# Softmax weights scaled in place and turned by TensorE's transpose mode, in place of products with diagonal matrices

## The chip, the cores and the metric

The kernel runs on one core of a Trainium2 chip. The metric is the device time of one execution, in microseconds (us), as the median over runs. The engines are named as the profile names them: PE is TensorE (PEld its weight loads), DVE is VectorE, ACT is ScalarE, POOL is GpSimd, SP is SyncE, which issues the DMAs.

## What is computed

The reference is one decoder layer on 512 tokens of width 1024, all in float32: a recurrent branch and a sparse-attention branch are merged by gates, and a convolutional feed-forward part and a gated embedding follow. The change touches the attention alone, whose core, cut, is

```python
logits = jnp.einsum('btngd,btknd->btngk', qg, k_sel).astype(jnp.float32) * (HEAD_DIM ** -0.5)
logits = logits + bias.astype(jnp.float32)
logits = jnp.where((dist >= 0)[:, :, None, None, :], logits, -jnp.inf)
probs = jax.nn.softmax(logits, axis=-1).astype(v.dtype)
o = jnp.einsum('btngk,btknd->btngd', probs, v_sel)
```

There are eight heads of 128 channels; four heads share one head of keys and values. Of the keys that are not later than a query only the 128 with the best index scores take part; the kernel keeps all 512 keys and adds a large negative mask to the others.

## The kernel before

Activations lie with channels on the 128 partitions and the 512 tokens along the free dimension. A weight matrix is streamed as tiles of 128x1024 (`load`, line 85) and split into a rounded part and a remainder (`split`, line 90: ACT casts `raw` to `whi`, DVE subtracts to `wlo`). Each product of two float32 matrices is then three passes in the reduced type float32r (`three`, line 97). A weight tile makes one output tile `acc` of 128x512 by 8 x 3 = 24 such products (`mm`, line 102); they are called wide products below. `pair` (line 112) splits an activation in the same way: ACT casts, DVE subtracts.

The attention is interleaved with these weight products. `attn(s)` hands to step s, ahead of its weight products, the turn of head s - 1 and the scores of head s, and in their midst the value product of head s - 1. The steps are the last three of the query projection and then those of the second gate (`b_step`, line 404, whose results `gb` get a sigmoid on ACT).

Per head there are these parts:

- `qk` (line 359). For each block b of 128 queries the scores against the 128(b + 1) keys up to it go to a PSUM tile `aux` (three products). DVE multiplies by the query's scale and adds the bias (line 369), then adds the mask and takes the row maximum (line 371), all into the tile `E`, in which the four blocks lie side by side with 128, 256, 384 and 512 columns. ACT takes the exponential with the negated maximum and sums the row (line 376); DVE takes the reciprocal of the sums (line 377). Line 380 then makes four diagonal matrices `dg`: the identity scaled, row by row, by these reciprocals.
- `turn` (line 382). The value product needs the weights with keys on the partitions. Each of the ten 128x128 blocks of `E` is loaded as the stationary operand and multiplied in float32 by the diagonal matrix of its query block, which turns it and normalises it at once. The results fill three PSUM tiles; `pair` splits them into `PT` (lines 115 and 116).
- `pv` (line 394). Twelve products of values and `PT`; `pair` writes the head's output into `QO`.

A scheduler sets the order of the instructions on each engine: it takes the program's order as priority and places an instruction where it takes its inputs to be ready. Every engine then works through its queue in that order. ACT loads a function table where the next function (exponential or sigmoid) is not in the loaded one. The tile `E` has two buffers, `dg` and `PT` have one, and PSUM has five tiles for `aux`.

The lines with two products per block are these:

```python
nc.tensor.matmul(a[:, c:c + 128], E[h][:, SEG[b] + 128 * j:SEG[b] + 128 * j + 128], dg[:, b],
                 start=True, stop=True)
```

Of the kernel before, what the change touches and what calls it, by code (L numbers as in the profile page):

```python
# [10 lines left out]
F32 = mybir.dt.float32  # L11
# [8 lines left out]
NB = 4  # L20
# [22 lines left out]
SEG = [0, 128, 384, 768]  # L43
# [4 lines left out]
def layer(ctx: ExitStack, tc: tile.TileContext, xT, pT, wall, vwi, vec, relb, onehot, out):  # L48
    nc = tc.nc
# [13 lines left out]
    ident = base.tile([128, 128], F32, name="ident")  # L63
# [10 lines left out]
    def aux_tile():  # L74
        return psum.tile([128, T], F32, name="aux", bufs=5)
# [21 lines left out]
    def three(o, lh, ll, rh, rl, start, stop):  # L97
        nc.tensor.matmul(o, lh, rh, start=start, stop=False)  # L98
        nc.tensor.matmul(o, lh, rl, start=False, stop=False)  # L99
        nc.tensor.matmul(o, ll, rh, start=False, stop=stop)  # L100
# [11 lines left out]
    def pair(dst, src, g=None, lo=None):  # L112

        if g is None:
            nc.scalar.copy(dst[:, 0], src)
            nc.vector.tensor_sub(dst[:, 1], src, dst[:, 0].bitcast(F32))
        else:
            nc.scalar.activation(dst[:, 0], src, AF.Copy, scale=g)
            nc.vector.scalar_tensor_tensor(dst[:, 1], src, g, dst[:, 0].bitcast(F32),
                                           op0=OP.mult, op1=OP.subtract)  # L120
# [42 lines left out]
    P = {}  # L163
# [180 lines left out]
        nc.scalar.activation(s, s, AF.Sqrt, bias=epsc[:, 1:2])  # L344
        nc.vector.reciprocal(s, s)

    G, E, DG, PT = {}, {}, {}, {}

    def spread_bias(h):
        nc.sync.dma_start(bias_d[h], bv_d[h:h + 1].to_broadcast([128, 640]))  # L350
# [8 lines left out]
    def qk(h):  # L359
        n = h // 4  # L360
        E[h] = P["pool"].tile([128, 1280], F32, name="E", bufs=2)
        sm = pm.tile([128, 4, 4], F32, name="sm", bufs=2)
        for b in range(NB):
            w = 128 * (b + 1)
            s = slice(b * 128, b * 128 + 128)
            a = aux_tile()[:, :w]
            three(a, QO[:, h, 0, s], QO[:, h, 1, s], KK[:, n, 0, :w], KK[:, n, 1, :w], True, True)
            e = E[h][:, SEG[b]:SEG[b] + w]
            nc.vector.scalar_tensor_tensor(e, a, qs[:, h, b:b + 1], G[h][:, 128 * (3 - b):128 * (3 - b) + w],
                                           op0=OP.mult, op1=OP.add)  # L370
            nc.vector.tensor_tensor_reduce(e, e, mask[:, SEG[b]:SEG[b] + w], 1.0, SENT, OP.add, OP.max,
                                           sm[:, 0, b:b + 1])
        nc.vector.tensor_scalar_mul(sm[:, 1], sm[:, 0], -1.0)
        for b in range(NB):
            e = E[h][:, SEG[b]:SEG[b] + 128 * (b + 1)]
            nc.scalar.activation(e, e, AF.Exp, bias=sm[:, 1, b:b + 1], accum_out=sm[:, 2, b:b + 1])
        nc.vector.reciprocal(sm[:, 3], sm[:, 2])
        DG[h] = P["pool"].tile([128, NB, 128], F32, name="dg", bufs=1)
        for b in range(NB):
            nc.vector.tensor_scalar_mul(DG[h][:, b], ident, sm[:, 3, b:b + 1])  # L380

    def turn(h):
        dg = DG[h]
        PT[h] = P["pool"].tile([128, 2, 1280], F32R, name="PT", bufs=1)
        for js, o, n in (((0,), 0, 512), ((1, 3), 512, 512), ((2,), 1024, 256)):
            a = aux_tile()
            for j in js:
                for b in range(j, NB):
                    c = PTO[j] - o + 128 * (b - j)
                    nc.tensor.matmul(a[:, c:c + 128], E[h][:, SEG[b] + 128 * j:SEG[b] + 128 * j + 128], dg[:, b],  # L390
                                     start=True, stop=True)
            pair(PT[h][:, :, o:o + n], a[:, :n])

    def pv(h):
# [232 lines left out]
    def attn(s):  # L627
        pre, ex = [], []
        if 0 <= s - 1 < HEADS:
            if s == 1:  # L630
                ex.append((4, lambda: turn(0)))
            else:
                pre.append(lambda: turn(s - 1))
            ex.append((6, lambda: pv(s - 1)))
        if 0 <= s < HEADS:
            pre.append(lambda: qk(s))
            ex.append((7, lambda: load_bias(s + 2)))
        return pre, ex
# [232 lines left out]
```

## Time and profile before

| | us |
|---|---|
| median of 3 runs | 949.13 |
| lowest and highest | 948.16, 949.47 |
| the profiled execution | 947.85 |
| its span, first to last instruction | 946.1 |
| PE busy | 931.9 |
| DVE busy | 575.1 |
| ACT busy | 435.4 |

A busy share is an average over the whole kernel. The place of the change is a stretch of some 90 us, from about 313 to 403 us. In a timeline each row has its start, its duration, engine, line, operation, tiles, shape and count; an "x20" merges 20 instructions that follow one another. A duration on PE reaches from the start of a product to its modelled end, which overlaps the next; the pace is read from the starts. A float32 product leaves two records, and a float32r product one.

### The profile page before, as it was taken

The page shows a single profiled execution, that of the slowest core. Times are in us where ns is not written, and L with a number is a line of the kernel's source. Part 1 is how long each engine was busy: PE and PEld are TensorE (multiplying, and loading weights), DVE is VectorE, ACT ScalarE, POOL GpSimd, SP SyncE. Part 2 cuts the span into 40 slices and gives each one's busy share as a digit, 9 for nine tenths or more (in the row PEclk, how much of TensorE's full clock was granted, in tenths as well). Part 3 has the DMA queues.
Part 4 walks back from the last instruction along what each step waited for, and adds up shares of the span by engine and source line. Part 5 has one row for each costly group of instructions (what it writes and reads, how often), then busy time and mean ns, then how long its engine had stood idle before and what let it go on. Part 6 is the DMA issues. An engine that isn't in the chain of part 4 may idle for free.

```text
span 946.1 us, 11256 instructions
## 1 busy us (share of the span) xinstructions
PE 931.9 (99%) x4332; PEld 776.9 (82%) x4332; DVE 575.1 (61%) x916; ACT 435.4 (46%) x624; POOL 40.5 (4%) x44
## 2 busy tenths in 40 slices
PE   7899999999999999999999999999999999999998
PEld 5788878888888888888888888888888888888886
DVE  6769699689983857735566555555555543332373
ACT  6557876995222557742344433333333322222341
POOL 2000000000000000000000111111111100000000
PEclk9999999999999999999999999999999999999999
DMA  7561123114333311123442323223223223223242
GB/s 266 175 223 52 65 89 116 63 68 134 112 112 94 118 45 56 46 89 95 150 133 97 104 90 102 99 89 105 96 89 109 92 89 111 90 90 111 100 144 89
DMA packets 31317, 99.31 MB, mean 105 GB/s; under 512 B 3480, under 2 KB 3992, under 8 KB 31264
## 3 DMA queue, kind: packets, MB, share of 16 engines
q1 hardware_dynamic: 31248, 98.58, 31.5%
q8 instruction: 34, 0.56, 0.3%
q14 instruction: 19, 0.16, 0.1%
q10 hardware_dynamic: 16, 0.02, 0.0%
HBM read 94.37 MB, written 6.84 MB: 107 GB/s over the span
## 4 chain that ended last, share of the span: by engine, by line
PE 93%; DVE 3%; ACT 3%; DMA 1%; issue 0%; SPq 0%; DVEq 0%
PE acc L98 28%; PE acc L100 28%; PE acc L99 28%; PE aux L390 2%; PE aux L98 1%; PE aux L100 1%; PE aux L99 1%; PE aux L337 1%; DMA F<-in_xT 1%; DVE rstd L426 1%; ACT ri L269 1%; DVE tmp L548 1%; DVE XN L554 0%; PE aux L214 0%; PE aux L213 0%
## 5 line engine op out<-in xcount | busy, mean ns | idle before, releaser
L94 ACT CAST whi<-raw 128x1024 fp32r<-128x1024 f32 (+1 forms) x157 | 164.2, 1046 | 360.0 <-PE acc L99 281.6
L95 DVE TENSOR_TENSOR wlo<-raw,whi 128x1024 fp32r<-128x1024 f32 (+1 forms) x157 | 191.0, 1217 | 96.3 <-ACT whi L94 95.1
L98 PE MATMUL acc<-XN,whi 128*128 128x512 f32 x504 | 197.4, 392 | 0.0
L100 PE MATMUL acc<-XN,wlo 128*128 128x512 f32 x504 | 196.9, 391 | 0.0
L99 PE MATMUL acc<-XN,whi 128*128 128x512 f32 x504 | 196.9, 391 | 0.0
L100 PE MATMUL acc<-XG,wlo 128*128 128x512 f32 (+1 forms) x456 | 175.8, 386 | 0.0
L98 PE MATMUL acc<-XG,whi 128*128 128x512 f32 (+1 forms) x456 | 175.8, 386 | 0.0
L99 PE MATMUL acc<-XG,whi 128*128 128x512 f32 (+1 forms) x456 | 175.8, 386 | 0.0
L100 PEld LDWEIGHTS acc<-XN,wlo 128*128 128x128 f32 x504 | 94.7, 188 | 20.7 <-DVE wlo L95 1.0
L98 PEld LDWEIGHTS acc<-XN,whi 128*128 128x128 f32 x504 | 94.7, 188 | 18.7
L99 PEld LDWEIGHTS acc<-XN,whi 128*128 128x128 f32 x504 | 94.7, 188 | 18.6
L99 PEld LDWEIGHTS acc<-XG,whi 128*128 128x128 f32 x456 | 85.7, 188 | 17.3
L98 PEld LDWEIGHTS acc<-XG,whi 128*128 128x128 f32 x456 | 85.7, 188 | 17.1
L100 PEld LDWEIGHTS acc<-XG,wlo 128*128 128x128 f32 x456 | 85.7, 188 | 17.0
L464 DVE TENSOR_TENSOR gp<-acc,rstd 128x512 f32<-128x512 f32 x24 | 16.6, 693 | 60.2 <-PE acc L100 60.1
L100 PE MATMUL acc<-H,wlo 128*128 128x512 f32 x128 | 49.8, 389 | 0.0
L98 PE MATMUL acc<-H,whi 128*128 128x512 f32 x128 | 49.8, 389 | 0.0
L99 PE MATMUL acc<-H,whi 128*128 128x512 f32 x128 | 49.8, 389 | 0.0
L477 DVE TENSOR_TENSOR tmp<-tmp,acc 128x512 f32<-128x512 f32 x24 | 16.5, 688 | 47.3 <-POOL tmp L470 47.3
L470 POOL TENSOR_TENSOR tmp<-tmp,rstd 128x512 f32<-128x512 f32 x24 | 30.8, 1282 | 273.5 <-ACT tmp L469 273.5
L469 ACT ACTIVATE tmp<-tmp 128x512 f32<-128x512 f32 x24 | 15.2, 632 | 47.1 <-DVE tmp L468 47.1
L468 DVE SCALAR_TENSOR_TENSOR tmp<-gp,vc,tmp 128x512 f32<-128x512 f32 x48 | 36.0, 749 | 0.8
(218 smaller groups left out, 1223.2 us busy)
## 6 DMA issues: line engine op xcount, KB each, us to landing
raw<-in_wall SPq DMA_DIRECT2D x154, 512.0 KB, 3.3
bias_d<-bv_d SPq DMA_DIRECT2D x8, 320.0 KB, 5.9
F<-in_xT SPq DMA_DIRECT2D x8, 256.0 KB, 5.4
proj_d<-pst SPq DMA_DIRECT2D x4, 512.0 KB, 3.7
bias<-bias_d SPq DMA_DIRECT2D x8, 256.0 KB, 2.7
tmp<-in_xT SPq DMA_DIRECT2D x8, 256.0 KB, 3.7
tmp<-proj_d SPq DMA_DIRECT2D x8, 256.0 KB, 3.4
out_dram<-tmp SPq DMA_DIRECT2D x7, 256.0 KB, 2.5
```

The source lines that it names most:

```text
L94: nc.scalar.copy(HI[i][:, :n], RAW[i][:, :n])
L95: LAST[0] = nc.vector.tensor_sub(LO[i][:, :n], RAW[i][:, :n], HI[i][:, :n].bitcast(F32))
L98: nc.tensor.matmul(o, lh, rh, start=start, stop=False)
L99: nc.tensor.matmul(o, lh, rl, start=False, stop=False)
L100: nc.tensor.matmul(o, ll, rh, start=False, stop=stop)
L269: nc.scalar.activation(dst[m], a, AF.Sigmoid, bias=col(b0 + m))
L390: nc.tensor.matmul(a[:, c:c + 128], E[h][:, SEG[b] + 128 * j:SEG[b] + 128 * j + 128], dg[:, b], start=True, stop=True)
L464: nc.vector.tensor_mul(gp[:, 2:], a, rstd)
L468: nc.vector.scalar_tensor_tensor(t, gp[:, j:j + T], col(V_FW + 24 * j + f), t, op0=OP.mult, op1=OP.add)
L469: nc.scalar.activation(t, t, AF.Gelu_apprx_tanh)
L470: nc.gpsimd.tensor_mul(t, t, rstd)
L477: nc.vector.tensor_mul(t, GL[f], a)
```

## The change

`qk` no longer makes diagonal matrices. It multiplies each block of `E` by the reciprocals in place. `turn` then uses TensorE's transpose mode with the constant identity.

```diff
         nc.vector.reciprocal(sm[:, 3], sm[:, 2])
-        DG[h] = P["pool"].tile([128, NB, 128], F32, name="dg", bufs=1)
         for b in range(NB):
-            nc.vector.tensor_scalar_mul(DG[h][:, b], ident, sm[:, 3, b:b + 1])
+            e = E[h][:, SEG[b]:SEG[b] + 128 * (b + 1)]
+            nc.vector.tensor_scalar_mul(e, e, sm[:, 3, b:b + 1])
 
     def turn(h):
-        dg = DG[h]
...
-                    nc.tensor.matmul(a[:, c:c + 128], E[h][:, SEG[b] + 128 * j:SEG[b] + 128 * j + 128], dg[:, b],
-                                     start=True, stop=True)
+                    nc.tensor.transpose(a[:, c:c + 128], E[h][:, SEG[b] + 128 * j:SEG[b] + 128 * j + 128], ident)
```

Since the scheduler places instructions anew, the order changes in the attention stretch on PE, DVE and ACT, and nowhere else but for tile numbers. Three places follow. In each fence a row is line, operation, output <- inputs, shape of the output and, after an x, how often it stands there in a row.

DVE, from the end of the scores of head 6 on; `sm` holds maxima, sums and reciprocals. Before:

```order
L373 TENSOR_SCALAR sm<-sm 128x4
L377 RECIPROCAL sm<-sm 128x4
L380 TENSOR_SCALAR dg<-ident,sm 128x128 x4
L116 TENSOR_TENSOR QO<-aux,QO 128x512
L95 TENSOR_TENSOR wlo<-raw,whi 128x1024
L116 TENSOR_TENSOR PT<-aux,PT 128x512
```

And with the change:

```order
L116 TENSOR_TENSOR QO<-aux,QO 128x512
L373 TENSOR_SCALAR sm<-sm 128x4
L377 RECIPROCAL sm<-sm 128x4
L380 TENSOR_SCALAR E<-E,sm 128x128
L380 TENSOR_SCALAR E<-E,sm 128x256
L380 TENSOR_SCALAR E<-E,sm 128x384
L380 TENSOR_SCALAR E<-E,sm 128x512
L95 TENSOR_TENSOR wlo<-raw,whi 128x1024
```

The four equal scalings have become four of growing width, and the remainder of the output of head 5 (`QO`) has moved from behind them to ahead of the negated maximum.

ACT, the exponentials of head 6. Before:

```order
L115 CAST PT<-aux 128x512
L115 CAST PT<-aux 128x256
L376 ACT_TABLE_LOAD
L376 ACTIVATE E,sm<-E,sm 128x128
L376 ACTIVATE E,sm<-E,sm 128x256
L376 ACTIVATE E,sm<-E,sm 128x384
L376 ACTIVATE E,sm<-E,sm 128x512
L115 CAST QO<-aux 128x512
```

And with the change:

```order
L115 CAST PT<-aux 128x512 x2
L115 CAST PT<-aux 128x256
L115 CAST QO<-aux 128x512
L376 ACT_TABLE_LOAD
L376 ACTIVATE E,sm<-E,sm 128x128
L376 ACTIVATE E,sm<-E,sm 128x256
```

The cast of the output of head 5 stands ahead of the table load, which it followed before.

PE, the turn of head 5. Before:

```order
L98 MATMUL acc<-XN,whi 128x512
L99 MATMUL acc<-XN,whi 128x512
L390 MATMUL aux<-dg,E 128x128 x10
L98 MATMUL aux<-KK,QO 128x128
L99 MATMUL aux<-KK,QO 128x128
```

And with the change:

```order
L100 MATMUL acc<-XN,wlo 128x512
L389 MATMUL aux<-ident,E 128x128 x3
L98 MATMUL acc<-XN,whi 128x512
L389 MATMUL aux<-ident,E 128x128 x7
L98 MATMUL aux<-KK,QO 128x128
```

One wide product has come in between the turned blocks. From here to the turn of head 6 there were 25 wide products and are now 31: one within the turn, two around the scores, and 28 behind the value product, where 14 stood.

## Rows read from the trace of the kernel before

**Rows 1.** The page, busy time of each engine.

```profile
PE 931.9 (99%) x4332; PEld 776.9 (82%) x4332; DVE 575.1 (61%) x916; ACT 435.4 (46%) x624; POOL 40.5 (4%) x44
```

**Rows 2.** Windows, one head: length, busy us (instructions) PE, PEld, DVE, ACT, POOL, clock, DMA.

```profile
366.60:378.35 11.75, 11.75 (x71) 10.49 (x71) 8.39 (x23) 8.71 (x18) 0.00 (x0) 1.00 0.13 46
```

**Rows 3.** Timeline of PE, from the turn of head 4 to that of head 5.

```profile
364.97 2.39 PE L390 MATMUL aux<-dg,E 128*128 128x128 f32 x20
367.12 0.30 PE L98 MATMUL aux<-KK,QO 128*128 128x128 f32 x1
...
371.63 0.39 PE L98 MATMUL aux<-PT,V 128*128 128x512 f32 x1
...
373.21 0.22 PE L98 MATMUL aux<-PT,V 128*128 128x128 f32 x1
373.26 0.28 PE L99 MATMUL aux<-PT,V 128*128 128x128 f32 x1
...
373.49 0.44 PE L98 MATMUL acc<-XN,whi 128*128 128x512 f32 x1
...
376.73 2.39 PE L390 MATMUL aux<-dg,E 128*128 128x128 f32 x20
```

**Rows 4.** Timeline of DVE in the same stretch; in brackets idle time and what ended it.

```profile
367.69 0.89 DVE L369 SCALAR_TENSOR_TENSOR E<-aux,qs,bias 128x128 f32<-128x128 f32 x2 [0.32 <-PE aux L100]
...
369.10 1.02 DVE L116 TENSOR_TENSOR PT<-aux,PT 128x512 fp32r<-128x512 f32 x2
370.04 1.27 DVE L369 SCALAR_TENSOR_TENSOR E<-aux,qs,bias 128x384 f32<-128x384 f32 x2
...
372.43 0.17 DVE L373 TENSOR_SCALAR sm<-sm 128x4 f32<-128x4 f32 x1
374.96 0.18 DVE L377 RECIPROCAL sm<-sm 128x4 f32<-128x4 f32 x1 [2.36 <-ACT E L376]
375.17 0.87 DVE L380 TENSOR_SCALAR dg<-ident,sm 128x128 f32<-128x128 f32 x4
```

**Rows 5.** Timeline of ACT in the same stretch.

```profile
369.35 1.28 ACT L376 ACT_TABLE_LOAD   x1
...
374.83 0.56 ACT L115 CAST QO<-aux 128x512 fp32r<-128x512 f32 x1
375.30 0.57 ACT L409 COPY gb<-acc 128x512 f32<-128x512 f32 x1
375.78 1.04 ACT L94 CAST whi<-raw 128x1024 fp32r<-128x1024 f32 x1
```

**Rows 6.** Timeline of PE, turn of head 0 and the statistics products behind it.

```profile
318.25 2.39 PE L390 MATMUL aux<-dg,E 128*128 128x128 f32 x20
320.48 0.95 PE L337 MATMUL aux<-ones,tmp 128*128 128x2 f32 x8
```

**Rows 7.** Groups by form, DVE, scalings by a column: busy us, mean ns of one.

```profile
L380 DVE TENSOR_SCALAR dg<-ident,sm 128x128 f32<-128x128 f32 x32 | 7.0, 282 | 0.2
...
L218 DVE TENSOR_SCALAR mask<-tmp,wi 128x512 f32<-128x512 f32 x1 | 0.5, 486 | 0.0
L218 DVE TENSOR_SCALAR mask<-tmp,wi 128x384 f32<-128x384 f32 x1 | 0.5, 451 | 0.0
...
L218 DVE TENSOR_SCALAR mask<-tmp,wi 128x256 f32<-128x256 f32 x1 | 0.4, 384 | 0.0
```

**Rows 8.** Timeline of PE at the start of the kernel.

```profile
9.01 0.63 PE L99 MATMUL acc<-QO,whi 128*128 128x512 f32 x1
9.44 0.63 PE L100 MATMUL acc<-QO,wlo 128*128 128x512 f32 x1
...
10.74 0.39 PE L98 MATMUL acc<-QO,whi 128*128 128x512 f32 x1
10.97 0.39 PE L99 MATMUL acc<-QO,whi 128*128 128x512 f32 x1
```

**Rows 9.** Timeline of DVE, the diagonal matrices of head 1.

```profile
323.26 0.87 DVE L380 TENSOR_SCALAR dg<-ident,sm 128x128 f32<-128x128 f32 x4
```

More of the change, by code (lines that the diff above doesn't have):

```diff
@@ L345, in q_scale @@
         nc.vector.reciprocal(s, s)
-    G, E, DG, PT = {}, {}, {}, {}
+    G, E, PT = {}, {}, {}
     def spread_bias(h):
```

## The prediction

> **What bounds the kernel now.** I read the page first: TensorE is busy 931.9 of 946.1 us [rows 1]. A change can therefore pay only by shortening TensorE's queue, and whatever it lays on another engine costs only where TensorE comes to wait for it. Next the stretch of the edited lines, the attention heads, which run from about 318 to 403 us between the ordinary weight products. The window view of one whole head [rows 2] shows TensorE busy 11.75 of 11.75 us at granted clock 1.00 (the 2.4 GHz level), VectorE 8.39, ScalarE 8.71. So a head lasts as long as its TensorE work. The timeline [rows 3] confirms it: the block turns of heads 4 and 5 start at 364.97 and 376.73, 11.76 apart, with nothing idle between them.
>
> What hides behind that is a chain which the reader should follow in [rows 4] and [rows 5]. A score product enters VectorE (367.69); the sums and maxima end with the negated maximum (372.43); ScalarE's exponentials take until the reciprocal (374.96, 2.53 later); the four diagonal tiles run from 375.17 to 376.04; the turn that needs them starts at 376.73. The spare time is 0.69 us, the number this change plays with.
>
> **The change, part by part.**
>
> *Products removed.* Ten 128x128 blocks a head are turned, and each costs two records today: 20 records from 376.73, and 2.15 us for the same 20 between 364.97 and 367.12 [rows 3], so 0.1075 us a record and 0.215 a block. The changed program, built, holds 4252 matmuls and as many weight loads, 80 of each fewer than the 4332 of [rows 1]: one pass for each of the 80 blocks instead of two. What such a pass costs no row shows. From above: 0.215, if one pass is as long as the two. From below: 0.055, the distance at which one 128-column product follows another (373.21 and 373.26, [rows 3]). In between lies the row that is most alike, today's own record: a new 128-column load for each product, 0.1075. That loads and not columns set that pace is seen in the statistics products, which stream two columns and still need 0.95 us for eight [rows 6]. I take 0.1075: 80 x (0.215 - 0.1075) = **8.6 us** off TensorE's queue, 1.08 a head.
>
> The Trainium skill, "TensorE: Matmul & The Clock Gate", section Terms, says that the transpose mode makes float32 four times faster. By it a block would cost an estimated 0.054 us and the term would be 12.9 us; the trace of before has no transpose that could confirm it.
>
> *Scaling moved.* The four diagonal tiles, 0.87 us a head [rows 4], go; four in-place scalings of 128, 256, 384 and 512 columns come. Their nearest rows are the scalings by a column of weights: 384, 451 and 486 ns at 256, 384 and 512 columns [rows 7]. With 0.28 for the narrow one that makes 1.60. Today's four of 0.282 end within 0.87, so they overlap by about 0.085 at each of three joints; less that, 1.35 us, 0.48 more than before. Lower bound: no growth. Upper bound: the pace of the two-input sums of the same widths, 0.89 + 1.27 [rows 4], 2.16 less overlap, about 1.93. VectorE has 3.4 us a head free [rows 2], so its load costs nothing; the 0.48 lies on the chain.
>
> *Order moved.* The scheduler puts the heads further apart: between the turns of heads 5 and 6 stand 31 wide products instead of 25, so a head's TensorE time becomes 11.76 - 1.08 + 6 x 0.23 = 12.06 us (0.23: 10.74 to 10.97, [rows 8]). Those products are only moved, not added. ScalarE now casts the attention output ahead of the exponentials and loads their table between the two. In before that load (369.35, 1.28 us [rows 5]) sat in idle time; now it is on the chain.
>
> *Where a wait could come.* I walk head 6 from the first turned block of head 5 (t = 0). The ten blocks and one wide product end at 1.31. VectorE takes the first score 0.57 after that product's start (367.12 to 367.69), at 1.88. Then come 1.41 for the narrow sums and maxima, 0.6 and 0.94 for the three PT remainders, 2.39 for the wide sums and maxima, 0.6 for the output's remainder [rows 4] (0.6 is my share for a 512-wide one of the two that take 1.02): 7.8. ScalarE: the value product ends 28 wide products before the next turn, 12.06 - 6.4 = 5.6; 0.2 until it is seen, 0.47 for the cast, 1.28 for the table: 7.6. So VectorE still ends last. The reciprocal comes 2.53 after the negated maximum, at 10.35; the scalings run from 10.55 to 11.9. The first block needs only the first scaling, and the fourth scaling is wanted some 0.3 after the turn's start at 12.06. **No wait**, with 0.4 spare. Heads 0 and 2 to 5 come out alike or looser.
>
> Two heads are late. Head 7: ScalarE has the output's cast and a gate copy, 0.95, a weight cast, 1.04 [rows 5], and then the table load ahead of its exponentials: 6.0 + 2.0 + 1.28 = 9.3, the reciprocal 2.4 later, the scalings to 13.2, where the turn (33 wide products, 12.5) wants the last at about 13.0: 0.2 us. Head 1: its diagonals (323.26, [rows 9]) move, with the maximum that they hang on, by the 0.48 of head 0's scalings, and its own take 1.35, so they end at 325.1. TensorE, from 318.25 with 1.08, 0.95, nine wide products (2.1) and the value products (1.86, 371.63 to 373.49), is at 324.2 and wants the fourth scaling at 324.5: 0.6 us.
>
> **Sum.** -8.6 + 0.2 + 0.6 = -7.8. The profiled execution took 947.85 us, which gives 940.05; the median of three runs is 1.28 above it, so in terms of that median **941.3 us**. The weight stream behind it (a split every 24 wide products) keeps its pace, since ScalarE has 3 us a head free [rows 2].
>
> **Rivals.**
>
> *The chain wins back part.* If the scalings run at the upper bound, 1.93, each lies 0.58 later. Head 1 gets it twice, 1.16; head 7 once; heads 2, 4, 5 and 6 exceed their 0.4 by some 0.2 each. The waits grow from 0.8 by 1.16 + 0.58 + 0.8 to about 3.3, and the time is 949.1 - 5.3 = 943.8. For it: the chain has 0.4 to spare in my walk, and each step has its error. Against: the scalings by a column [rows 7] are far below the two-input pace.
>
> *A cheaper pass.* At 0.055 a block 12.8 us go; TensorE then runs into the chain at five heads, some 0.15 each, and 1.6 of waits in all leave -11.2: 937.9. For it: columns do pass at this distance where the load is ready [rows 3]. Against: ten blocks have ten different loads, the pace of today's 20 records. It is the case to which the sentence of the Trainium skill on the transpose mode (Terms, above) would lead.
>
> *It does not do what it says.* One pass in transpose mode takes 0.215: nothing is saved, TensorE is slower again against the chain, and 0 to 0.8 of waits remain: 949.5. For it: no row of before has the mode. Against: half the loads are gone.
>
> *Slower: the clock.* At the kernel's start the first wide products stand 0.43 apart (9.01, 9.44), a few products later 0.23 (10.74, 10.97) [rows 8]: 512 columns at the 1.2 and at the 2.4 GHz level. If turned blocks do not keep the engine at the upper level, each wide product behind them costs 0.20 more, and from 39 of these on (five a head) the gain is gone. Were it so from each turn to the end of its value products, some 4.5 us a head, the cost is 36 us: 977. The Trainium skill, same page, Part 4, says of the transpose mode that the full clock "doesn't engage" for it, and so speaks for this case. Against: a turn lasts 1.1 us and has 6 us of ordinary products on either side, and heads at full clock already hold 2.15 us of slow-paced records [rows 2, 3].
>
> **How the numbers follow.** Forecast 0.60, the chain 0.18, the cheaper pass 0.10, no saving 0.07, the clock 0.05. The range runs from the cheaper pass, 937.9, to 945.5, which holds the chain's case and 1.7 us more of waits; no saving and the clock are outside. No change means within 0.2%, 1.9 us. Faster by more: 0.60 + 0.18 + 0.10 = 0.88. Same: 0.05 of the no-saving case. Slower: the clock's 0.05 and the 0.02 of no saving in which its waits are larger, 0.07.
>
> **What would show it.** Right: 80 records on the transposing line at starts 0.11 apart, ten within about 1.1 us; scalings of 1.3 to 1.4 us a head; TensorE idle ahead of the turns of heads 1 and 7 only, under 1 us in all; wide products 0.23 apart behind each turn. Wrong: 0.2 between blocks (no saving), 0.06 (cheaper pass), TensorE waiting for scalings at every head (the chain), 0.4 between wide products (the clock). The prediction fails most likely in the walk: if ScalarE's table loads fall elsewhere than I have put them, each wrong head moves it by up to 1.3 us.

## The result, and the profile after

The changed kernel takes **941.32 us** (median of four runs, 939.93 to 942.34) beside 949.30 us for the kernel before in the same job (948.16 to 949.47): a ratio of 0.9917, 95% interval 0.990 to 0.9935. The forecast was 941.3 in a range of 937.9 to 945.5. In the last job, on another occasion, the two stood at 941.07 and 949.26, ratio 0.9912 (0.9898 to 0.9925).

The page of the changed kernel, span and busy time of each engine:

```profile
span 939.7 us, 11073 instructions
...
PE 924.9 (98%) x4252; PEld 768.8 (82%) x4252; DVE 576.2 (61%) x916; ACT 435.8 (46%) x624; POOL 40.5 (4%) x44
```

Against [rows 1] TensorE has 80 matmuls and 80 weight loads less and 7.0 us less busy time; VectorE and ScalarE have what they had. The two profiled spans differ by 6.4 us only, and the medians by 8.0, because this execution came later to the first statistics product, the first record of line 337: at 125.68 us, in before at 123.89. Its first matmul began at 6.11 us instead of 5.04, and between 30 and 35 us TensorE was granted 0.73 of its clock, where before had 1.00. Both vary between runs of one and the same kernel. In e6 and c2 below, two profiled runs of one kernel, the first matmul began at 5.37 and at 5.60 us, but the first statistics product came at 127.87 and at 124.15. What sets these two apart is mostly the clock: at the products of line 526 e6 is 0.8 us behind c2 (15.54 and 14.72), at the next wide product 3.2 (21.24 and 18.08). Windows of e6 and then of c2 (length, busy us of PE, PEld, DVE, ACT, POOL, then the clock):

```profile
15.00:20.00 5.00, 4.46 (x16) 3.89 (x17) 3.65 (x8) 3.21 (x6) 0.00 (x0) 0.59 0.35 106
20.00:25.00 5.00, 5.00 (x22) 4.30 (x22) 2.76 (x3) 2.52 (x5) 2.65 (x2) 0.73 0.72 260
```

```profile
15.00:20.00 5.00, 5.00 (x30) 4.18 (x31) 4.07 (x9) 4.11 (x9) 0.91 (x1) 1.00 0.56 166
20.00:25.00 5.00, 4.36 (x25) 3.56 (x23) 5.00 (x4) 2.07 (x4) 4.22 (x3) 1.00 0.52 189
```

All this lies far ahead of the edited lines. So for what follows I use a length without the start, **from the first statistics product to the end of the span**, and call it the run behind the start. It is 946.1 - 123.89 = 822.21 us before and 939.7 - 125.68 = 814.02 us after, **8.19 us less**. A second trace of the changed kernel gave 813.86.

Now the turned blocks. This is the view of the transposing line, with load and product apart; the three numbers are the shortest, middle and longest record in ns:

```profile
L389 PEld LDWEIGHTS aux<-ident,E x80: 137/140/146, 319.8 to 404.2; 128*128 128x128 f32 x80
L389 PE MATMUL aux<-ident,E x80: 270/272/329, 320.0 to 404.3; 128*128 128x128 f32 x80
...
its engine sat idle before it (us, times) until:
  DVE E L380: 0.7, 2
  issue: 0.4, 1
```

And TensorE's timeline: the turns of heads 0, 1 and 3 with the product behind the last, and the first pieces of those of heads 5 and 6:

```profile
320.01 1.25 PE L389 MATMUL aux<-ident,E 128*128 128x128 f32 x10
...
326.15 1.51 PE L389 MATMUL aux<-ident,E 128*128 128x128 f32 x10
...
353.33 0.27 PE L389 MATMUL aux<-ident,E 128*128 128x128 f32 x1
353.35 0.48 PE L100 MATMUL acc<-XN,wlo 128*128 128x512 f32 x1
353.67 1.14 PE L389 MATMUL aux<-ident,E 128*128 128x128 f32 x9
354.57 0.31 PE L98 MATMUL aux<-KK,QO 128*128 128x128 f32 x1
...
378.19 0.49 PE L389 MATMUL aux<-ident,E 128*128 128x128 f32 x3
...
390.27 0.27 PE L389 MATMUL aux<-ident,E 128*128 128x128 f32 x1
```

Ten blocks take 1.25 us, where twenty records took 2.39 [rows 3]. The last record's own 0.27 set aside, that is 0.98 / 9 = 0.109 us a block, beside 2.12 / 19 = 0.112 a record before. Head 3's turn, split by one wide product, takes 354.57 - 353.33 = 1.24 us to the next score product, less 0.23 for the wide one 1.01; before, that stretch was 2.15. Either way a turn is 1.14 us shorter. The turns of heads 5 and 6 start 12.08 apart. Head 1's turn is 0.26 longer than head 0's: it waits for a scaling.

VectorE's side of it, in the groups by form (busy us, mean ns of one), and in the timeline at head 6:

```profile
L380 DVE TENSOR_SCALAR E<-E,sm 128x512 f32<-128x512 f32 x8 | 3.8, 480 | 0.0
L380 DVE TENSOR_SCALAR E<-E,sm 128x384 f32<-128x384 f32 x8 | 3.3, 414 | 0.0
L380 DVE TENSOR_SCALAR E<-E,sm 128x256 f32<-128x256 f32 x8 | 2.8, 347 | 0.0
```

```profile
385.77 0.15 DVE L373 TENSOR_SCALAR sm<-sm 128x4 f32<-128x4 f32 x1
388.29 0.18 DVE L377 RECIPROCAL sm<-sm 128x4 f32<-128x4 f32 x1 [2.36 <-ACT E L376]
388.50 1.28 DVE L380 TENSOR_SCALAR E<-E,sm 128x128 f32<-128x128 f32 x4
```

The four scalings of a head take 1.28 us together (the diagonals took 0.87, [rows 4]). The waits of TensorE's loads between 310 and 410 us (in all, how often, the longest):

```profile
PEld aux L389 <- DVE E L380: 0.7, 2, 0.4
PEld aux L98 <- DVE PT L116: 0.6, 2, 0.5
PEld aux L389 <- issue: 0.4, 1, 0.4
```

Three more waits of 0.2 us each follow in that view; before, these loads waited for 0.8 us in all. The scalings are waited for at heads 1 and 4. The wait put down to issue is that of the first load of head 7's turn: it started at 402.90, and the first scaling had ended at 402.78, so I count it with them. So here is where the 8.19 us come from: eight turns lost 1.14 us each, 9.1 us. The 0.9 that is missing is put down to waits by difference; not every wait of a load delays a product, so the list above does not add up to it.

### The profile page after: what moved, and what is told of

Read it like the earlier page. It is cut to its first block, busy times and chain, and to the rows that moved or that the text cites. A ratio compares the mean times of both kernels' runs of the same rounds, so it can differ in the third digit from the quotient of the medians.

```text
span 939.7 us, 11073 instructions
## 1 busy us (share of the span) xinstructions
PE 924.9 (98%) x4252; PEld 768.8 (82%) x4252; DVE 576.2 (61%) x916; ACT 435.8 (46%) x624; POOL 40.5 (4%) x44
## 4 chain that ended last, share of the span: by engine, by line
PE 93%; DVE 3%; ACT 3%; DMA 1%; issue 0%; SPq 0%; DVEq 0%
PE acc L98 28%; PE acc L99 28%; PE acc L100 28%; PE aux L98 1%; PE aux L100 1%; PE aux L99 1%; PE aux L389 1%; PE aux L337 1%; DMA F<-in_xT 1%; DVE rstd L424 1%; ACT ri L269 1%; DVE tmp L546 1%; DVE XN L552 0%; PE aux L214 0%; PE aux L213 0%
## 5 line engine op out<-in xcount | busy, mean ns | idle before, releaser
L98 PEld LDWEIGHTS acc<-XN,whi 128*128 128x128 f32 x504 | 94.7, 188 | 18.4
L98 PE MATMUL acc<-QO,whi 128*128 128x512 f32 x76 | 31.0, 408 | 6.1 <-ACT whi L762 6.1
```

## The experiments

All edits are to the changed kernel. Some expectations below count "from record 1000 to the end", which is the same measure as the run behind the start, 100.0 us shorter (714.0 and 722.2 for the two kernels). In e7, e9 and c3 fewer matmul records stand ahead of that record, which shifts such a count, so the results are given for the run behind the start. Each one is to be compared with 814.0 for the changed kernel and 822.2 for the kernel before; the two traces of each kernel that was profiled twice agree within 0.3 us. The times of e3, e4, e5 and e8 are of one execution; the kernel before stood at 950.0 us in the first job (e1, e3, e4, e5) and at 950.3 in the second (e2, e6, e8, e9).

| run | run behind the start, us | against the changed kernel | time, us |
|---|---|---|---|
| before | 822.21 | +8.2 | 949.3 |
| changed, again (c1) | 814.02, 813.86 | 0 | 941.3, 941.1 |
| e1 ordinary product with the identity | 823.10 | +9.1 | 950.5 |
| e4 every transpose twice | 823.95 | +9.9 | 951.4 |
| e8 half the columns, twice the records of e1 | 841.50 | +27.5 | 969.0 |
| e2 one-pass product, float32r | 820.86 | +6.8 | 948.4 |
| e3 no scaling | 814.88 | +0.9 | 941.3 |
| e5 scaled twice | 815.38 | +1.4 | 943.9 |
| e6, c2 blocks by query | 814.03, 813.75 | 0 | 942.4, 941.8 |
| e7 one-pass statistics | 813.02 | -0.9 | 939.7 |
| e9, c3 both of these | 812.66, 812.64 | -1.3 | 941.5, 939.4 |

### Is it the passes?

**e1: the scalings stay, the transpose mode goes.**

```diff
-nc.tensor.transpose(a[:, c:c + 128], E[h][...], ident)
+nc.tensor.matmul(a[:, c:c + 128], E[h][...], ident, start=True, stop=True)
```

> The scalings in place stay, but each block is turned by an ordinary float32 product with the identity (two passes, 160 records) instead of the transpose mode. Theory (the gain is the dropped pass): the 80 passes come back at 0.1075 us each, +8.6 us; with twenty records a turn the chain of VectorE and ScalarE has about 1 us a head more to spare, so the waits of about 1.1 us that the changed kernel has go. The stretch from head 0's first score product to the first product of the output projection, 96.77 us in the changed kernel, becomes 104.3 to 105.4, and the time 949 to 950 us, no change against the kernel before. Rival (the gain came from the new order or from the scalings, not from the passes): the stretch stays near 97 and the time near 941.

Measured: 950.49 us, 1.0007 of the kernel before (0.9997 to 1.0017); +9.1 us behind the start. Eight turns with 2.39 in place of 1.25 us make 9.1. The theory had 7.5 to 8.6: a turn gives back 1.14 and not 1.08, and the waits did not go. The scalings in place have no gain of their own; the gain is the dropped pass. Compared with before e1 is even 0.9 us longer by the run behind the start; TensorE's loads wait for 1.6 us from 226 us to the end, where they wait for 0.8 before. So the moved scaling and the order that goes with it cost about what the prediction had put down for waits. It is not the changed kernel's order, though: the scheduler places e1 anew, with 26 wide products between the turns of heads 3 and 4 where the changed kernel has 32.

**e4: a second transpose of each block.**

```diff
 nc.tensor.transpose(a[:, c:c + 128], E[h][...], ident)
+nc.tensor.transpose(a[:, c:c + 128], E[h][...], ident)
```

> Every transpose is issued twice, 160 records in transpose mode, same output. Theory (a pass costs what the loads pace, about 0.11 us in transpose mode too): +80 x 0.11 = +8.8 us, less the waits of about 1.1 us that the longer turns cover: the stretch of 96.77 us becomes 104.2 to 105.6. Rival (a second pass that follows on the first is cheaper in transpose mode, or the turn is not what TensorE is paced by): under +6 us.

Measured: +9.9 us. Head 3's turn, first and last of its twenty records:

```profile
355.42 0.27 PE L389 MATMUL aux<-ident,E 128*128 128x128 f32 x1
...
357.49 0.27 PE L390 MATMUL aux<-ident,E 128*128 128x128 f32 x1
```

2.07 us for 19 steps is 0.109 a pass, so 80 of them are 8.7 us. The other 1.2 are mostly waits: TensorE sat idle for 1.03 us of 310 to 425 us, where the changed kernel has 0.10. My theory had those waits shrinking behind longer turns. They grew, mostly for the remainders of the weights and of the outputs (line 116), which a longer turn delays.

**e8: the columns halved, the loads doubled.**

```diff
-nc.tensor.transpose(a[:, c:c + 128], E[h][...], ident)
+for z in (0, 64):
+    nc.tensor.matmul(a[:, c + z:c + z + 64], E[h][...], ident[:, z:z + 64], start=True, stop=True)
```

> Each block is turned by two ordinary float32 products with the two halves of the identity, 64 columns each: 320 records, every one with its own load of a 128 x 128 block, and the same columns in all as the 160 records of the run with the ordinary identity products (723.1 us from record 1000 to the end). Theory (the load in front of each record sets its pace, not the columns): 0.09 to 0.11 us a record all the same, so +160 x 0.09 to 0.11 = +14 to +18 us on 723.1, some 737 to 741 us. Rival (the columns set it): 0.055 a record, no change, 723 us.

Measured: 841.50, 18.4 us over e1 with the same columns in all. A turn:

```profile
320.07 4.57 PE L390 MATMUL aux<-ident,E 128*128 128x64 f32 x40
```

(4.57 - 0.27) / 39 = 0.110 us a record, though each streams 64 columns instead of 128: 160 more records at 0.110 are 17.6. Behind head 0's turn the clock fell for a while as well (last section). So a record that brings a new load takes 0.10 to 0.11 us whether it streams 2 columns ([rows 6]), 64 or 128. That is the step on which I had chosen 0.1075 between 0.055 and 0.215, and it holds.

Nor is it a fixed price of a product. The products at 373.21 and 373.26 in [rows 3] start 0.055 us apart, but their loads do not:

```profile
373.08 0.19 PEld L98 LDWEIGHTS aux<-PT,V 128*128 128x128 f32 x1
373.21 0.19 PEld L99 LDWEIGHTS aux<-PT,V 128*128 128x128 f32 x1
373.32 0.19 PEld L100 LDWEIGHTS aux<-PT,V 128*128 128x128 f32 x1
```

The first of the two products had to wait for a product of 256 columns ahead of it (373.08), and the second followed at once; the third came 0.12 later. In the whole trace of before no two loads start less than 0.108 us apart, though products do. The changed kernel has five pairs of transposing loads 0.057 to 0.063 us apart, each in a turn that was held up or broken by another product, and none in the undisturbed turn of head 0.

**e2: one pass without the transpose mode.** The weights are rounded to float32r on the way.

```diff
+ER[h] = P["pool"].tile([128, 1280], F32R, name="ER", bufs=1)
-nc.vector.tensor_scalar_mul(e, e, sm[:, 3, b:b + 1])
+nc.vector.tensor_scalar_mul(ER[h][:, g], E[h][:, g], sm[:, 3, b:b + 1])
-nc.tensor.transpose(a[:, c:c + 128], E[h][...], ident)
+nc.tensor.matmul(a[:, c:c + 128], ER[h][...], P["ident_r"], start=True, stop=True)
```

> The scalings write the weights out of place, rounded to float32r (fewer mantissa bits than float32), and each block is turned by one ordinary float32r product with an identity in float32r: one pass, 80 records, no transpose mode. From record 1000 to the end of the span the changed kernel takes 714.0 us, the kernel before 722.2. Theory (it is the number of passes that counts, whatever the mode): 80 records at about 0.11 us, ten within 1.2 us, 714.0 give or take 1 us for other waits; time 940 to 943 us. Rival (the transpose mode itself is the faster way, as its shorter load records of 140 against 192 ns could mean): 0.05 us a record more, 80 x 0.05 = 4 us, 718 us. Rival (a float32r product of 128 columns passes at the 0.055 of the score products): 80 x 0.055 = 4.4 us less, 709.6 us.

Measured: the records are as the theory has them, the time is not: 948.4 us, 0.9983 of before (0.9972 to 0.9994).

```profile
L390 PEld LDWEIGHTS aux<-identr,ER x80: 186/192/192, 318.8 to 404.1; 128*128 128x128 f32 x80
...
338.75 1.23 PE L390 MATMUL aux<-identr,ER 128*128 128x128 f32 x10
```

Ten in 1.23 us: one pass is 0.107 us in this mode as well, though its load record lasts 192 ns and not 140. So it is the number of passes and not the mode, and the shorter load record buys nothing here. But the order is not the changed kernel's: from the turn of head 3 on, 26, 28, 32 and 27 wide products stand from turn to turn, as in e1, where the changed kernel has 32, 32, 31 and 33. With turns 1.1 us shorter than those of e1, TensorE came to wait for remainders. Waits of PE's products, from 226 us to the end:

```profile
PE aux L98 <- DVE PT L116: 1.6, 2, 1.2
PE aux L98 <- DVE QO L116: 0.9, 1, 0.9
PE aux L98 <- ACT PT L115: 0.4, 2, 0.2
```

With them 3.06 us of 310 to 425 us stood idle, and for some 3 us the clock fell (last section), which cost about 1.5. The rest of the +6.8 I have not split up. The time alone would have spoken for the rival of 4 us; only the records tell the two apart.

### Is the chain the bound?

**e3: no scaling.** Left out are the reciprocal and the four scalings, so the weights are not divided by their row sums.

```diff
-nc.vector.reciprocal(sm[:, 3], sm[:, 2])
-for b in range(NB):
-    e = E[h][:, SEG[b]:SEG[b] + 128 * (b + 1)]
-    nc.vector.tensor_scalar_mul(e, e, sm[:, 3, b:b + 1])
```

> Left out: the reciprocal and the four scalings of every head, so the weights go on without the division by their row sums. TensorE has the same records. Theory (TensorE sets the pace, the chain shows only in the waits ahead of some turns): the stretch of 96.77 us gets shorter by those waits alone, 0.6 to 1.4 us. Rival (the chain of VectorE and ScalarE has become the bound, as in the chain's case of the prediction): 1.4 us a head less on the chain brings at least 3 us, up to 8 x 1.4 = 11.

Measured: +0.9 us, longer and not shorter, which neither side had. The waits from 226 us to the end:

```profile
PEld aux L98 <- DVE PT L116: 1.6, 3, 0.7
PEld aux L385 <- ACT E L376: 1.2, 5, 0.3
PEld aux L98 <- DVE QO L116: 0.8, 1, 0.8
```

With 1.5 us taken from the chain the scheduler moved the heads closer together (the turns of heads 3 to 7 start 10.8 to 12.0 us apart, instead of 12.1 to 12.7), and TensorE waits for the exponentials instead, at five turns, and for remainders. The chain is not the bound. Nor was the wait at head 1 or 4 a loss that a shorter chain wins back: another took its place. (This run and the next are one trace each, and two traces of one kernel differ by up to 0.3 us.)

**e5: every scaling twice.** The second multiplication changes the output.

```diff
 nc.vector.tensor_scalar_mul(e, e, sm[:, 3, b:b + 1])
+nc.vector.tensor_scalar_mul(e, e, sm[:, 3, b:b + 1])
```

> Each block row is scaled twice in place (the second multiplication changes the output). The chain gets 1.2 to 1.4 us longer at every head, TensorE's records stay. Theory (the chain has 0.4 to 2 us to spare at most heads, none at heads 1, 4 and 7): waits grow by about 1.2 at three heads, twice that at head 1, and by 0.3 to 0.8 at the others: the stretch grows by 4 to 7 us, with TensorE waiting for VectorE's scalings at nearly every turn. Rival (the chain has much more to spare than the walk says): under 2 us. Rival (the chain binds already): 8 x 1.3 = 10 us or more.

Measured: +1.4 us for 8 x 1.2 us more on the chain: the first rival. Head 3's turn shows why:

```profile
356.01 0.49 PE L390 MATMUL aux<-ident,E 128*128 128x128 f32 x3
...
357.28 0.93 PE L390 MATMUL aux<-ident,E 128*128 128x128 f32 x7
```

The turn is split, three blocks first, then four wide products, then seven, at seven of the eight heads. The scheduler saw the longer scalings and put other work in their place. The spare time of 0.4 us in my walk was not the chain's real reserve, since the order isn't fixed.

### Versions that might be faster still

**e6: blocks by query**, the fourth scaling's blocks last.

```diff
-for js, o, n in parts:
-    a = aux_tile()
-    for j in js:
-        for b in range(j, NB):
-            nc.tensor.transpose(...)
-    pair(PT[h][:, :, o:o + n], a[:, :n])
+a = [aux_tile() for _ in parts]
+for b in range(NB):
+    for z, (js, o, n) in enumerate(parts):
+        for j in js:
+            if j <= b:
+                nc.tensor.transpose(...)
+for z, (js, o, n) in enumerate(parts):
+    pair(PT[h][:, :, o:o + n], a[z][:, :n])
```

> The turn's ten transposes are issued by query block, so the four that need the fourth scaling come last (in the changed kernel the first of them is the fourth), and the three PSUM tiles are opened together. Theory (1.1 us of waits at turns of heads 1, 4, 5 and 7 come from the fourth scaling): these waits shrink, since the fourth scaling is wanted 0.3 us later: 714.0 us from record 1000 to the end becomes 713.2 to 713.8. Rival (the remainders of PT, which now all start only after the last transpose, come late for the value products): +0.3 to +1.5 us.

> The turn's blocks by query, again. Its first run took 0.9 us less than the changed kernel behind the same record, but its profiled execution had come to that record 3 us later, and its median was no shorter. Theory (the late start is the jitter of the first loads): the median is 0.5 to 1.5 us below that of the changed kernel beside it. Rival (the start is later in this program at every execution): no shorter, or 1 to 2 us longer.

Measured: no gain. 942.43 us, and beside the changed kernel 941.78 against 941.07. The 0.9 us of the second expectation was a miscount: from the same record on, both traces take 714.0; behind the start the two traces are at 814.03 and 813.75. The late start of e6 was no property of the program: c2 is the same program and came to the first statistics product 3.7 us earlier. Waits put down to scalings fell from 0.7 to 0.4 us, those for the remainders of the attention weights rose from 0.6 to 0.9. The theory had the fourth scaling behind the waits, and in the changed kernel that is so at head 1 alone, where the load at 326.68 follows a fourth scaling that ended at 326.62. At heads 4 and 7 the first load of the turn, at 365.72 and 402.90, waits for the first scaling, which ended at 365.67 and 402.78. No order of the blocks helps there, and e6 has both waits still, 0.4 us each.

**e7 and e9: the query statistics in one pass** (their squares rounded to float32r), alone and with e6.

```diff
-nc.scalar.activation(q2, a, AF.Square)
+nc.scalar.activation(q2.bitcast(F32R), a, AF.Square)
-nc.tensor.matmul(s[...], q2[...], ones[:, :2], ...)
+nc.tensor.matmul(s[...], q2[...].bitcast(F32R), ones_r[:, :2], ...)
```

> The query order of the turn, and the products that sum the squares of the queries (32 float32 products of two passes, 64 records) made float32r (the squares rounded to float32r when they are written): one pass, 32 records. Theory (it is passes that cost, 0.10 us each at the pace of those records): 32 x 0.10 = 3.2 us less than the run with the query order alone, and so about 710.3 us from record 1000 to the end, 937.5 to 938.5 us in time, faster than both kernels. Rival (the chain of VectorE and ScalarE has become the bound): the saved passes turn into waits ahead of the turns, under 1.5 us are gained.

> Query order and one-pass statistics, again; in its first run 1.3 us less than the changed kernel behind the record at which the heads' work begins, where 4 had been expected. Theory (jitter of the start): the median is 1 to 4 us below that of the changed kernel beside it. Rival (the start is later in this program at every execution): within 1 us of it.

> The one-pass statistics alone, with the changed kernel's turn. Theory (32 records at 0.10 us, less the waits that come in their place): 1 to 3.2 us below the changed kernel beside it. Rival (other waits take all of it): within 1 us.

> The changed kernel as it is, beside the two variants of this call on the same chip. Both theories: 941 to 943 us, 0.992 of the kernel before; it is the measure for the next two.

Measured: a group of statistics products falls from 0.95 to between 0.50 and 0.61 us, so about 3 us of TensorE's queue are gone, but only 1.3 (e9, c3) and 0.9 (e7) arrive. That is the size of e9's rival, but the waits that take the rest are not those ahead of the turns. In c3, from 30 to 320 us and from there to 425 us, TensorE waits for more of what feeds those products and the weight stream:

```profile
PEld aux L337 <- ACT tmp L332: 1.7, 4, 1.0
PEld acc L100 <- DVE wlo L95: 1.5, 2, 0.9
...
PEld aux L337 <- ACT tmp L332: 0.9, 1, 0.9
```

The changed kernel has 1.3, 0.6 and nothing there. In time c3 has 939.39 us, 0.9891 of before (0.9876 to 0.9906), e7 939.67, beside 941.07 and 0.9912 (0.9898 to 0.9925) for the changed kernel. The intervals overlap; the traces behind the start are the better evidence for a small gain, which costs the precision of the squares.

## Why the prediction was right, point by point

- **What bounds the kernel.** Right for the turns. Passes put back come back in full (e1, e4); 1.2 us more or 1.5 us less on the chain a head change the run behind the start by +1.4 and +0.9 us (e5, e3). It is not a law of the kernel: of the statistics passes, on the same engine, less than half arrived (e7, e9).
- **One pass a block at 0.1075 us.** Right: 0.109, with the bounds of 0.055 and 0.215 both far off. The term itself came out at 9.1 instead of 8.6, since 2.15 us for 20 records averages in the hand-over to the next product, which is 0.03; a step inside the turn is 0.112, and a turn of ten records fewer is 1.14 shorter, not 1.08. e8 shows that columns do not set the pace: half the columns, same 0.11. The lower bound was not a pace at all: the loads of its two products stand 0.13 apart (shown at e8).
- **A rule weighed.** The Trainium skill, "TensorE: Matmul & The Clock Gate", section Terms, has transposes of float32 four times faster. This trace differs: against the two-pass product of before the block went from 0.223 to 0.109 us, half, and a one-pass product without the mode passes at 0.107. The forecast by the row of before was nearer than one by that sentence.
- **Scalings of 1.35 us a head.** 1.28 measured, 0.07 less: a little below the weight scalings that the estimate took (480, 414, 347 ns at 512, 384 and 256 columns against 486, 451 and 384 in [rows 7]). The upper bound of 1.93 takes off too much overlap, since 0.89 and 1.27 are each the length of two instructions together; 2.08 would have been right, and the measured value is below both.
- **The walk.** Head 6: reciprocal forecast at 10.35 behind head 5's turn, measured 388.29 - 378.19 = 10.10; scalings' end forecast at 11.9, measured 11.59; next turn forecast at 12.06, measured 12.08. No wait, as forecast.
- **Waits.** Forecast at head 1 (0.6) and head 7 (0.2); there are 0.3 and 0.4, and 0.4 at head 4, which the words "heads 0 and 2 to 5 come out alike or looser" missed. There ScalarE has a gate's copy and its sigmoid (360.28 and 360.90, 0.6 each) ahead of the table load, and the reciprocal comes 4.15 after the negated maximum instead of 2.52. At heads 4 and 7 the turn waits for the first scaling, where the walk of head 7 had the last. Waits for scalings sum to 1.1 where 0.8 stood; by the run's length the new waits cost 0.9. That this sum came out is in part luck: head 1's overestimate and the missed head 4 stand against each other in it.
- **The sum.** -7.8 forecast, -8.19 in the traces: 0.5 more from the passes, 0.1 more in waits. That the median meets the forecast of 941.3 to the tenth is luck: the four runs lie 2.4 us apart, and the median of before moved by 0.17 between the two measurements.
- **The rivals.** The cheaper pass and no saving are excluded by 0.109. The chain was overpriced: it took the order as fixed, and e5 shows that a lengthening of 1.2 a head costs 1.4 us in all, where I gave 2.5 to one of 0.58. The clock did not fall behind the turns of the changed kernel: the granted clock is 1.00 from 310 to 425 us, and wide products behind the turns stand 0.23 apart (355.34 and 355.57). The twenty transposes a turn of e4 left it at 1.00 as well. In e2 and e8, whose turns are ordinary products, it did fall behind one turn each; what brought it there stays open, below.

## What to carry to other kernels

Count the weight loads when each product brings a new one: at 0.11 us apiece they were the price here, whether 2, 64 or 128 columns followed, and a float32 product in two passes pays twice. A busy share of 98% does not say what a removed pass is worth. For the turns 8.2 of 9.1 us arrived; for the statistics products, where TensorE then waited for inputs, 0.9 to 1.3 of 3. What was laid on the engines beside TensorE cost little as long as the scheduler had other products to put in front. For the same reason the spare time of one schedule is no price: an edit of a microsecond re-deals the order, and waits come back at another place.

## What the runs showed that was not expected

**A shorter load that saves nothing.** In transpose mode the load record lasts 140 ns (137 to 146), for the ordinary products of the same block 192. The records follow at 0.109 and 0.107 to 0.112 us all the same.

**The clock.** In eleven of the fourteen profiled runs the granted clock, after the slow first products ([rows 8]), fell again somewhere between 15 and 37 us, far ahead of the turns; it did not in before, c2 and e2. Behind turned blocks it fell twice. In e2 the granted clock of TensorE was 0.65 in the stretch from 391 to 394 us. Windows of e2 (length, busy us of PE, PEld, DVE, ACT, POOL, then clock) and its PE timeline there:

```profile
388.00:391.00 3.00, 3.00 (x20) 2.33 (x18) 1.56 (x6) 2.97 (x5) 0.00 (x0) 1.00 0.10 41
391.00:394.00 3.00, 2.54 (x9) 2.08 (x8) 3.00 (x10) 1.57 (x3) 0.00 (x0) 0.65 0.00 0
394.00:400.00 6.00, 6.00 (x29) 5.12 (x28) 3.88 (x9) 3.38 (x6) 0.00 (x0) 0.89 0.00 1
```

```profile
391.64 0.48 PE L98 MATMUL aux<-KK,QO 128*128 128x384 f32 x1 [0.46 <-DVE PT L116]
...
392.98 0.63 PE L99 MATMUL aux<-KK,QO 128*128 128x512 f32 x1
393.40 0.63 PE L100 MATMUL aux<-KK,QO 128*128 128x512 f32 x1
```

512 columns 0.42 us apart is the 1.2 GHz level, as at the kernel's start [rows 8]. Ahead of it stood a turn that lasted 1.78 us, six narrow score products and an idle time of 0.46 us. In e8 the clock went down behind head 0's turn, 4.57 us and the 1.00 of the statistics products:

```profile
326.00:328.00 2.00, 2.00 (x6) 1.55 (x5) 1.37 (x6) 0.82 (x3) 0.00 (x0) 0.50 0.00 0
```

It did not behind e8's turns of the same 4.57 us at heads 2 to 4, nor behind the longer idle times of e2 (0.92 at 328.50, 1.16 at 342.35). So what decides it stays open. The slower case of the prediction is not refuted for every order of this kernel, but the turns of the changed kernel did not bring it on; where the clock fell, it lasted for some nine products and cost about 1.5 us.
